# Queries and keys of a forgetting attention as pairs of float16, scaled by powers of two, on one core

## The chip, the core and the metric

The kernel runs on one core of one Trainium2 chip. The metric is the device time of one execution in microseconds (us). A core has five engines with a queue of instructions each: TensorE (PE, matmuls into PSUM), VectorE (DVE), ScalarE (ACT), GpSimd (POOL) and SyncE (SP, which issues DMAs here). An engine takes its instructions in order and waits on semaphores for the others.

## The reference

One layer for 2048 tokens of width 1024. A projection of the modulated RMSNorm gives queries, keys and values of 8 heads of 64 columns, a forget logit for each head, and the inputs of a gated short convolution. The change touches the attention alone:

```python
    q = rmsnorm(q.reshape(b, s, ATTN_HEADS, HEAD_DIM), q_norm_g)
    k = rmsnorm(k.reshape(b, s, ATTN_HEADS, HEAD_DIM), k_norm_g)
    logf = jax.nn.log_sigmoid((fg + b_forget).astype(jnp.float32))
    ...
    fcum = jnp.cumsum(logf, axis=1)            # per head
    for i in range(s // BLOCK_Q):              # 16 blocks of 128 queries
        logits = jnp.einsum('bqhd,bkhd->bhqk', qb, kb).astype(jnp.float32) * scale
        logits = logits + fcum[:, :, q0:q1, None] - fcum[:, :, None, :q1]
        logits = jnp.where(causal[None, None], logits, -jnp.inf)
        p = jax.nn.softmax(logits, axis=-1).astype(v.dtype)
        outs.append(jnp.einsum('bhqk,bkhd->bqhd', p, vb))
```

After it come the output projection, a second norm, and a feed-forward layer with a convolution (`w_up` to 5632 columns, `w_down` back).

## The kernel before

Everything is held to float32 accuracy by pairs: a number is split into a high part and the rest, both in a 4-byte matmul type (float32r), and a product is made of three matmuls, high by high, high by rest, rest by high (`mm3`, L139).

**Projections** (about 40 to 620 us of the span). The values come first. Then `project` runs twice, for the keys and for the queries. It goes over 16 tiles of 128 tokens: 24 matmuls (8 slices of the width, three each), then a norm for each head on ACT and DVE. `finish` of a tile comes two tiles later: PE transposes the tile (L462), ACT multiplies with the gain `gq` into `tf` (L468), POOL copies it to the high part `th`, DVE subtracts to get the rest `tl`, and SP stores both in DRAM (`k_hi`, `k_lo`, `q_hi`, `q_lo`). Small steps hang on the tiles as `hooks`: `running_sum` and `running_offset` for the cumulated forget gates (`cum`, stored as `nf_sc`), `largest_value` and `value_scale` for the scale of the values. After the queries come the convolution's projections (`pr`).

**Attention** (626 to about 970 us). `load_head` fetches a head: the keys' high part (`kh`) and rest (`kl`), 64 partitions each, which POOL copies to the other 64 partitions, and the queries' two parts, one above the other in `qs`; so one matmul with `qs` as the loaded weights gives high and rest of the queries at once. The work goes by units: one head and two query blocks, number 15 - u and u, for u from 0 to 7, which have 17 key blocks of 128 together. There are 64 units. For a unit

- `product` makes the scores on PE in chunks of up to 512 columns, five for a unit: one matmul with `kh` (L658), one with `kl` (L659), and for the last chunk of a block the causal mask (L661). It always issues two chunks at a time (GROUP), across the units;
- `scores` adds the forget term `nf` on DVE and finds the running maximum (L682, the output is `s_t`, 17 blocks wide);
- `weights` makes the bias `nb` from the maximum (L696) and takes the exponential of the two blocks on ACT, with their sums (L699);
- `turn` splits the result in two f16 parts and transposes it: seven key blocks by POOL (`wide`) and a transposing DMA (`far`), ten by PE (L719, into two PSUM buffers `pt`), ACT (`near`, L721) and DVE (`near`, L726);
- `values` multiplies with the values in f16 (L751 to L753), 64 columns a matmul, and ACT scales the result (`at`, L757).

The loop at the end of the part advances four units by one step each in turn: `turn` of the unit two before, `scores` of this one, `weights` of the one before, `values` of the one four before. PE, ACT and DVE are pinned to the order that is written so (`K`); SP's queue is placed by the framework.

Of the kernel before, what the change touches and what calls it, by code (L numbers as in the profile page):

```python
# [19 lines left out]
P = 128  # L20
S = 2048
D = 1024
H = 8
DH = 64
AW = 512
# [7 lines left out]
LN_PS = 9.704060527839234  # L33
# [11 lines left out]
def kernel(  # L45
# [19 lines left out]
    nc = tc.nc  # L65
    V, A, G, T = nc.vector, nc.scalar, nc.gpsimd, nc.tensor
# [4 lines left out]
    const = ctx.enter_context(tc.tile_pool(name="const", bufs=1))  # L71
# [5 lines left out]
    q_lo = dram.tile([P, 4, S], F32, name="q_lo")  # L77
    k_hi = dram.tile([P, 4, S], F32, name="k_hi")
    k_lo = dram.tile([P, 4, S], F32, name="k_lo")
# [66 lines left out]
    with ExitStack() as ph:  # L146
# [256 lines left out]
        def running_offset():  # L403
            po = ps_t.tile([P, 512], F32, tag="tr", name="po")
            K(T.matmul(po[:, 0:1], lhsT=blk.rearrange("p h t -> p (h t)"), rhs=cum[:, P - 1 : P], start=True, stop=True))
            off = bp.tile([P, 1], F32, name="off", bufs=1)
            V.tensor_copy(off, po[:, 0:1])
            V.tensor_scalar(cum, cum, off, -1.0, op0=ALU.add, op1=ALU.mult)
            nc.scalar.dma_start(nf_sc.rearrange("h (t k) -> (h t) k", k=P), cum)

        vr = bp.tile([1, 1], F32, name="vr", bufs=1)

# [43 lines left out]
        def project(col, gain, dst_hi, dst_lo, hooks):  # L456
            w = [w_slice(w_in[k * P : (k + 1) * P, col : col + AW], [P, AW]) for k in range(KD)]

            def finish(i, qn):
                pt = ps_t.tile([P, 512], F32, tag="tr", name="pt")  # L460
                for j in range(4):
                    K(T.transpose(  # L462
                        pt[:, j * P : (j + 1) * P], qn[:, 2 * j : 2 * j + 2, :].rearrange("p h d -> p (h d)"), ident
                    ))
# [3 lines left out]
                A.activation(tf, pt, AF.Copy, scale=gain)  # L468
                pool_copy(th, tf)
                V.tensor_tensor(tl, tf, th.bitcast(F32), op=ALU.subtract)  # L470
                for dst, src in ((dst_hi, th), (dst_lo, tl)):
                    nc.sync.dma_start(
                        dst[:, :, i * P : (i + 1) * P], src.bitcast(F32).rearrange("p (j n) -> p j n", j=4)
                    )

            normed = []
            for i in range(NT):
                ch, t = divmod(i, 4)
                acc = ps_m.tile([P, 512], F32, tag="mm", name="acc")
                for k in range(KD):  # L480
                    ah, al = h_hi[k][ch][:, t * P : (t + 1) * P], h_lo[k][ch][:, t * P : (t + 1) * P]
                    mm3(acc, ah, al, w[k][0], w[k][1], k == 0, k == KD - 1)
                    if k == MID and len(normed) == 2:
                        finish(*normed.pop(0))
                a3 = acc.rearrange("p (h d) -> p h d", d=DH)
                sq = bp.tile([P, 512], F32, tag="z", name="sq")
                A.activation(sq, acc, AF.Square)
# [12 lines left out]
            def finish_last():  # L500
                finish(*normed.pop(0))
                if col == 0 and not normed:
                    value_tiles(NT)

            return finish_last
# [44 lines left out]
                taken[1] += 1  # L550

        taken = [0, 0]
        last_k = project(AW, gq[:, 1:2], k_hi, k_lo, {3: running_sum, 5: running_offset, 7: largest_value, 9: value_scale})
        last_q = project(0, gq[:, 0:1], q_hi, q_lo, {0: last_k, 1: last_k, 3: piece, 6: piece, 9: piece, 12: piece, 15: piece})

        def load_head(h):

            pr, r0 = h // 2, (h % 2) * DH
            r1 = r0 + DH
            tiles, steps = [], []  # L560
            load = lambda *a: steps.append(lambda: nc.sync.dma_start(*a))
            for tag, srcs in (("kh", (k_hi,)), ("qs", (q_hi, q_lo)), ("kl", (k_lo,))):
                t = sp.tile([P, S], F32R, tag=tag, name=tag)
                for n, src in enumerate(srcs):
                    load(t.bitcast(F32)[n * DH : (n + 1) * DH, :], src[r0:r1, pr, :])
                tiles.append(t)
            t = sp.tile([P, S], F32, tag="nf", name="nf")
            load(t, nf_sc[h].partition_broadcast(P))
            for k in (tiles[0], tiles[2]):
                steps.append(lambda k=k: K(G.tensor_scalar(k[DH:P, :], k.bitcast(F32)[0:DH, :], 1.0, 0.0, op0=ALU.mult, op1=ALU.add)))  # L570
            return (*tiles, t), steps


# [47 lines left out]
    with ExitStack() as ph:  # L621
# [70 lines left out]
        def weights(un):  # L692

            s_t = un["s"]
            nb = cs.tile([P, 2], F32, tag="nb", name="nb")
            K(A.activation(nb, un["mx"], AF.Copy, scale=-1.0, bias=LN_PS))  # L696
            for p, (_, n, b0) in enumerate(un["parts"]):
                cols = s_t[:, b0 * P : (b0 + n) * P]
                K(A.activation(cols, cols, AF.Exp, bias=nb[:, p : p + 1], accum_out=un["l"][:, p : p + 1]))  # L699
# [492 lines left out]
```

## Time and profile before

| | |
|---|---|
| median of 3 runs | 2540.8 us (2540.46 to 2541.75) |
| the profiled execution | 2540.43 us, its span from first to last instruction 2538.7 us |
| PE, DVE, ACT, POOL busy | 2454.4, 1823.9, 1169.9, 359.4 us |
| granted clock of TensorE, mean | 0.993 |
| attention, 620 to 970 us of the span | PE 341.3, DVE 297.1, ACT 293.9, POOL 210.0 us busy |

An engine is busy while one of its instructions runs. Matmuls are pipelined: a row gives the time from a matmul's start to its modelled end, and the next one starts before that, so the rate is read from the starts. `<-` behind an idle time names what ended it.

### The profile page before, as it was taken

What the parts mean: (1) busy time and instruction counts of PE and PEld (TensorE: products, weight loads), DVE (VectorE), ACT (ScalarE), POOL (GpSimd) and SP (SyncE); (2) the same over time, 40 slices, a digit from 0 to 9 for tenths busy, and PEclk for the clock granted to TensorE, in tenths of its full rate; (3) what the DMA queues carried; (4) which work ended last, traced back from release to release, by engine and by line L of the source; (5) the groups of instructions that cost most, each with busy time, mean ns of one, the idle gap of its engine ahead of it and who ended that gap; (6) DMA issues with size and microseconds to landing.
All of it is one profiled execution on the core that took longest, in us unless ns stands there. A gap on an engine that the chain in (4) does not pass through costs nothing.

```text
span 2538.7 us, 38468 instructions
## 1 busy us (share of the span) xinstructions
PE 2454.4 (97%) x14490; PEld 2027.5 (80%) x14490; DVE 1823.9 (72%) x3282; ACT 1169.9 (46%) x1932; POOL 359.4 (14%) x314
## 2 busy tenths in 40 slices
PE   4999999999999997998999999999999999999999
PEld 4988788887788886876888888877778888888887
DVE  7567874433888886676888888667768888885554
ACT  3532331111888885654444444455534444444333
POOL 4210111101666655110000000000000000000000
PEclk9999999999999999999999999999999999999999
DMA  7433673325799867143222222676642222226775
GB/s 233 147 107 102 195 224 98 98 63 148 140 198 193 165 130 245 63 150 103 75 84 83 83 83 83 209 229 213 223 136 78 83 84 83 83 85 198 228 234 184
DMA packets 400290, 358.21 MB, mean 141 GB/s; under 512 B 133776, under 2 KB 310248, under 8 KB 397032
## 3 DMA queue, kind: packets, MB, share of 16 engines
q1 hardware_dynamic: 392920, 338.91, 46.6%
q10 hardware_dynamic: 4752, 8.46, 0.9%
q0 software_dynamic: 2432, 8.39, 0.9%
q8 instruction: 113, 1.85, 0.3%
q14 instruction: 73, 0.60, 0.1%
HBM read 252.86 MB, written 73.47 MB: 129 GB/s over the span
## 4 chain that ended last, share of the span: by engine, by line
PE 49%; DVE 2%; DMA 1%; ACT 1%; issue 0%; SPq 0%; ACTq 0%; DVEq 0%
PE acc L1044 33%; PE acc L139 16%; DMA t<-x_sc 1%; DVE lo L843 1%; PE pt L932 0%; DVE t L852 0%; DVE t L925 0%; DVE t L851 0%; ACT junk L955 0%; ACT hi L842 0%; DMA raw<-y_sc 0%; DVE b22l L843 0%; DVE lo L999 0%; DVE t L942 0%; ACT t L934 0%
## 5 line engine op out<-in xcount | busy, mean ns | idle before, releaser
L139 PE MATMUL acc<-hi 128*128 128x512 f32 x960 | 378.0, 394 | 15.9 <-ACT hi L842 12.3
L139 PE MATMUL acc<-hi,lo 128*128 128x512 f32 x960 | 375.7, 391 | 0.2 <-DVE lo L843 0.2
L139 PE MATMUL acc<-lo,hi 128*128 128x512 f32 x960 | 374.9, 391 | 0.0
L843 DVE TENSOR_TENSOR lo<-raw,hi 128x1024 fp32r<-128x1024 f32 (+1 forms) x208 | 236.0, 1141 | 182.5 <-ACT hi L842 182.2
L842 ACT ACTIVATE hi<-raw 128x1024 fp32r<-128x1024 f32 (+1 forms) x208 | 205.0, 991 | 247.7 <-PE acc L139 203.0
L1057 DVE SCALAR_TENSOR_TENSOR w<-w,fcw,w 128x1024 f32<-128x1024 f32 x176 | 225.9, 1283 | 35.5 <-ACT w L1052 32.2
L996 ACT ACTIVATE hi<-raw 128x1024 fp32r<-128x1024 f32 x132 | 139.7, 1060 | 213.4 <-PE acc L1044 204.7
L139 PEld LDWEIGHTS acc<-hi 128*128 128x128 f32 x960 | 180.9, 188 | 56.5 <-ACT hi L842 13.2
L139 PEld LDWEIGHTS acc<-hi,lo 128*128 128x128 f32 x960 | 180.6, 188 | 39.9 <-DVE lo L843 2.0
L139 PEld LDWEIGHTS acc<-lo,hi 128*128 128x128 f32 x960 | 180.9, 188 | 36.7 <-DVE lo L843 0.4
L999 DVE TENSOR_TENSOR lo<-raw,hi 128x1024 fp32r<-128x1024 f32 x132 | 160.9, 1220 | 11.0 <-ACT hi L996 10.9
L699 ACT ACTIVATE s_t<-s_t,nb 128x2048 f32<-128x2048 f32 (+15 forms) x128 | 152.9, 1196 | 5.7
L139 PE MATMUL pr<-hh,wh 128*128 128x512 f32 x384 | 153.3, 399 | 0.0
L139 PE MATMUL pr<-hl,wh 128*128 128x512 f32 x384 | 151.1, 393 | 0.0
L139 PE MATMUL pr<-hh,wl 128*128 128x512 f32 x384 | 150.8, 393 | 0.0
L726 DVE TENSOR_TENSOR near<-pt,near 128x512 f16<-128x512 f32 (+1 forms) x192 | 114.8, 599 | 44.7 <-ACT near L721 43.8
L658 PE MATMUL ps<-kh,qs 128*128 128x512 f32 (+1 forms) x320 | 133.6, 418 | 1.0 <-issue 0.8
L682 DVE CUSTOM_DVE_ANT_0 s_t<-ps,nf,mx 128x512 f32<-128x512 f32 (+1 forms) x192 | 123.2, 641 | 3.0 <-PE pt L719 0.4
L711 POOL TENSOR_TENSOR wide<-s_t,wide 128x896 f16<-128x896 f32 x64 | 121.7, 1901 | 5.3
L659 PE MATMUL ps<-kl,qs 128*128 128x512 f32 (+1 forms) x320 | 115.5, 365 | 0.0
L719 PE MATMUL pt<-ident,s_t 128*128 128x128 f32 x640 | 101.0, 283 | 7.6 <-DVE near L726 5.3
L139 PE MATMUL acc<-wh,hh 128*128 128x512 f32 x256 | 103.4, 404 | 0.0
(287 smaller groups left out, 6263.8 us busy)
## 6 DMA issues: line engine op xcount, KB each, us to landing
raw<-in_w_up_dram SPq DMA_DIRECT2D x88, 512.0 KB, 3.6
raw<-y_sc SPq DMA_DIRECT2D x176, 256.0 KB, 3.9
raw<-in_w_down_dram SPq DMA_DIRECT2D x176, 256.0 KB, 4.2
y_sc<-w SPq DMA_DIRECT2D x44, 512.0 KB, 2.6
wm<-in_w_ada_dram SPq DMA_DIRECT2D x128, 128.0 KB, 2.3
wr<-in_w_in_dram SPq DMA_DIRECT2D x40, 256.0 KB, 4.0
x_t<-in_x_dram SPq DMA_DIRECT2D x16, 512.0 KB, 5.4
wa<-in_w_ada_dram SPq DMA_DIRECT2D x16, 512.0 KB, 6.4
```

The source lines that it names most:

```text
L139: ins = T.matmul(acc, lhsT=a, rhs=b, start=st, stop=sp)
L658: K(T.matmul(ps[:, 0:cw], lhsT=qt, rhs=kh[:, c0 : c0 + cw], start=True, stop=False))
L659: K(T.matmul(ps[:, 0:cw], lhsT=qt, rhs=kl[:, c0 : c0 + cw], start=False, stop=not last))
L682: K(V.tensor_tensor_reduce(out=s_t[:, o0 + c0 : o0 + c0 + cw], in0=ps[:, 0:cw], in1=nf[:, c0 : c0 + cw], scale=1.0, scalar=-3.0e38 if g == ...
L699: K(A.activation(cols, cols, AF.Exp, bias=nb[:, p : p + 1], accum_out=un["l"][:, p : p + 1]))
L711: K(G.tensor_tensor(wide[:, 1, :], s_t[:, WB * P : WU], wide[:, 0, :], op=ALU.subtract))
L842: A.activation(hi, raw, AF.Copy, scale=HS)
L843: V.tensor_tensor(lo, raw, hi.bitcast(F32), op=ALU.subtract)
L996: K(A.activation(hi, raw, AF.Copy, scale=HS))
L999: K(V.tensor_tensor(lo, raw, hi.bitcast(F32), op=ALU.subtract))
L1044: K(T.matmul(acc, lhsT=a, rhs=b, start=st, stop=sp, skip_group_check=True))
L1057: K(V.scalar_tensor_tensor(y, u[:, m : m + 1024], fcw[:, m * 44 + ct : m * 44 + ct + 1], y, op0=ALU.mult, op1=ALU.add))
```

## The change

Queries and keys are kept as pairs of float16. Each gain is multiplied by a power of two that is found from the largest gain, and the product of the two scales is multiplied into the forget term. The logits stay scaled, and the exponential divides by the product of the scales, held in `qk`: column 4 is its reciprocal, column 5 the negative of that, column 3 the product.

```diff
-    q_hi = dram.tile([P, 4, S], F32, name="q_hi")
+    q_hi = dram.tile([P, 4, S], F16, name="q_hi")
...
+    qk = const.tile([P, 6], F32, name="qk")
...
             V.tensor_scalar(cum, cum, off, -1.0, op0=ALU.add, op1=ALU.mult)
+            V.tensor_scalar(cum, cum, qk[:, 3:4], None, op0=ALU.mult)
...
+        def largest_gains():
+            pt = ps_t.tile([P, 512], F32, tag="tr", name="pt")
+            K(T.transpose(pt[0:2, 0:P], gq, ident))
+            V.tensor_reduce(gm[:, 0:1], pt[0:2, 0:P], axis=AX.X, op=ALU.max, apply_absolute_value=True)
+            V.tensor_scalar(gm, ident[0:2, 0:2], gm[:, 0:1], 8.0, op0=ALU.mult, op1=ALU.mult)
+
+        def gain_scales():
+            pt = ps_t.tile([P, 512], F32, tag="tr", name="pt")
+            K(T.matmul(pt[:, 0:2], lhsT=ones[0:2, :], rhs=gm, start=True, stop=True))
+            s = qk[:, 0:2]
+            V.tensor_scalar(s, pt[:, 0:2], 2.0**-10, 2.0**60, op0=ALU.max, op1=ALU.min)
+            V.tensor_scalar(s.bitcast(I32), s.bitcast(I32), 0x7F800000, None, op0=ALU.bitwise_and)
+            V.reciprocal(s, s)
+            V.tensor_scalar(s.bitcast(I32), s.bitcast(I32), 0x7F800000, None, op0=ALU.bitwise_and)
+            V.tensor_scalar(s, s, 16384.0, None, op0=ALU.mult)
+            V.tensor_tensor(gq, gq, s, op=ALU.mult)
+            V.tensor_tensor(qk[:, 3:4], s[:, 0:1], s[:, 1:2], op=ALU.mult)
+            V.reciprocal(qk[:, 4:5], qk[:, 3:4])
+            V.tensor_scalar(qk[:, 5:6], qk[:, 4:5], -1.0, None, op0=ALU.mult)
...
-                th = bp.tile([P, 512], F32R, tag="th", name="th")
-                tl = bp.tile([P, 512], F32R, tag="tl", name="tl")
+                th = bp.tile([P, 512], F16, tag="th", name="th")
+                tl = bp.tile([P, 512], F16, tag="tl", name="tl")
...
-        last_k = project(AW, gq[:, 1:2], k_hi, k_lo, {3: running_sum, 5: running_offset, 7: largest_value, 9: value_scale})
+        last_k = project(AW, gq[:, 1:2], k_hi, k_lo, {0: largest_gains, 1: gain_scales, 3: running_sum, 5: running_offset, 7: largest_value, 9: value_scale})
...
-                t = sp.tile([P, S], F32R, tag=tag, name=tag)
+                t = sp.tile([P, S], F16, tag=tag, name=tag)
...
-            K(A.activation(nb, un["mx"], AF.Copy, scale=-1.0, bias=LN_PS))
+            K(A.activation(nb, un["mx"], AF.Copy, scale=qk[:, 5:6], bias=LN_PS))
...
-                K(A.activation(cols, cols, AF.Exp, bias=nb[:, p : p + 1], accum_out=un["l"][:, p : p + 1]))
+                K(A.activation(cols, cols, AF.Exp, bias=nb[:, p : p + 1], scale=qk[:, 4:5], accum_out=un["l"][:, p : p + 1]))
```

`q_lo`, `k_hi` and `k_lo` become float16 as `q_hi` does, and the stores and loads follow. The program's instructions stand as follows. First PE at the start of the attention, before and now:

```order
L658 MATMUL ps<-kh,qs 128x512
L659 MATMUL ps<-kl,qs 128x512
L658 MATMUL ps<-kh,qs 128x128
L659 MATMUL ps<-kl,qs 128x128
L661 LDWEIGHTS ident_b
L661 MATMUL ps<-maskb,ident_b 128x128
```

```order
L682 LDWEIGHTS qs
L682 MATMUL ps<-kh,qs 128x512
L683 LDWEIGHTS qs
L683 MATMUL ps<-kl,qs 128x512
L682 LDWEIGHTS qs
L682 MATMUL ps<-kh,qs 128x128
L683 LDWEIGHTS qs
L683 MATMUL ps<-kl,qs 128x128
L685 LDWEIGHTS ident_b
L685 MATMUL ps<-maskb,ident_b 128x128
```

No matmul moved; the load of the weights stands as an instruction of its own, 640 of them in all. Next ACT in the first unit of the attention, before and now:

```order
L696 ACTIVATE nb<-mx 128x2
L699 ACTIVATE s_t,l<-s_t,nb 128x2048
L699 ACTIVATE s_t,l<-s_t,nb 128x128
L721 ACTIVATE near<-pt 128x512 x2
L696 ACTIVATE nb<-mx 128x2
```

```order
L720 ACTIVATE nb<-mx,qk 128x2
L723 ACTIVATE s_t,l<-s_t,nb,qk 128x2048
L723 ACTIVATE s_t,l<-s_t,nb,qk 128x128
L745 ACTIVATE near<-pt 128x512 x2
L720 ACTIVATE nb<-mx,qk 128x2
```

The order is the same, and each of the three reads `qk` besides. Last SP, where the second next head is fetched between the transposing DMAs, before and now:

```order
L712 DMA_TRANSPOSE far<-wide 128x14x128 x6
L561 DMA kh<-k_hi 64x2048
L712 DMA_TRANSPOSE far<-wide 128x14x128
L561 DMA qs<-q_hi 64x2048
L712 DMA_TRANSPOSE far<-wide 128x14x128
L561 DMA qs<-q_lo 64x2048
L561 DMA kl<-k_lo 64x2048
```

```order
L736 DMA_TRANSPOSE far<-wide 128x14x128 x6
L585 DMA kh<-k_hi 64x2048
L585 DMA qs<-q_hi 64x2048
L736 DMA_TRANSPOSE far<-wide 128x14x128
L585 DMA qs<-q_lo 64x2048
L585 DMA kl<-k_lo 64x2048
```

The load of `q_hi` and what follows it stand one transpose earlier; later the stores of the attention's output stand one place later in turn. On POOL the copy of the first head's `kl` stands one instruction (`y`, L614) earlier. DVE has twelve instructions more, those of the diff, in the key projection.

More of the change, by code (lines that the diff above doesn't have):

```diff
@@ L74 @@
     dram = ctx.enter_context(tc.tile_pool(name="dram", bufs=1, space=DRAM))
-    q_hi = dram.tile([P, 4, S], F32, name="q_hi")
-    q_lo = dram.tile([P, 4, S], F32, name="q_lo")
-    k_hi = dram.tile([P, 4, S], F32, name="k_hi")
-    k_lo = dram.tile([P, 4, S], F32, name="k_lo")
+    q_hi = dram.tile([P, 4, S], F16, name="q_hi")
+    q_lo = dram.tile([P, 4, S], F16, name="q_lo")
+    k_hi = dram.tile([P, 4, S], F16, name="k_hi")
+    k_lo = dram.tile([P, 4, S], F16, name="k_lo")
     v_sc = dram.tile([S, AW], F32, name="v_sc")
@@ L408, in running_offset @@
             V.tensor_scalar(cum, cum, off, -1.0, op0=ALU.add, op1=ALU.mult)
+            V.tensor_scalar(cum, cum, qk[:, 3:4], None, op0=ALU.mult)
             nc.scalar.dma_start(nf_sc.rearrange("h (t k) -> (h t) k", k=P), cum)
+        gm = bp.tile([2, 2], F32, name="gm", bufs=1)
+        def largest_gains():
[16 more added lines that the diff above has]
+            V.tensor_scalar(qk[:, 5:6], qk[:, 4:5], -1.0, None, op0=ALU.mult)
         vr = bp.tile([1, 1], F32, name="vr", bufs=1)
@@ L562, in load_head @@
             for tag, srcs in (("kh", (k_hi,)), ("qs", (q_hi, q_lo)), ("kl", (k_lo,))):
-                t = sp.tile([P, S], F32R, tag=tag, name=tag)
+                t = sp.tile([P, S], F16, tag=tag, name=tag)
                 for n, src in enumerate(srcs):
-                    load(t.bitcast(F32)[n * DH : (n + 1) * DH, :], src[r0:r1, pr, :])
+                    load(t[n * DH : (n + 1) * DH, :], src[r0:r1, pr, :])
                 tiles.append(t)
@@ L569, in load_head @@
             for k in (tiles[0], tiles[2]):
-                steps.append(lambda k=k: K(G.tensor_scalar(k[DH:P, :], k.bitcast(F32)[0:DH, :], 1.0, 0.0, op0=ALU.mult, op1=ALU.add)))
+                steps.append(lambda k=k: K(G.tensor_scalar(k[DH:P, :], k[0:DH, :], 1.0, 0.0, op0=ALU.mult, op1=ALU.add)))
             return (*tiles, t), steps
```

6 lines of the change are left out of this document (2 added, 4 removed).

## The prediction

> **What bounds the kernel now.** I read the page first: the share of each engine, then the costliest groups, to find what the changed lines carry.
>
> ```profile
> span 2538.7 us, 38468 instructions
> PE 2454.4 (97%) x14490; PEld 2027.5 (80%) x14490; DVE 1823.9 (72%) x3282; ACT 1169.9 (46%) x1932; POOL 359.4 (14%) x314
> ```
>
> TensorE (PE) is busy for 97% of the span, ScalarE (ACT) for 46%. That is an average. The products of queries and keys stand in the attention alone, so the second view is the table by stretches there. I took 48 of its 64 units (a unit is one pair of query blocks of one head), from one `nb` instruction to the same one six heads later, and the waits in the same stretch.
>
> ```profile
> 670.20 0.21 ACT L696 ACTIVATE nb<-mx 128x2 f32<-128x2 f32 x1
> 925.74 0.21 ACT L696 ACTIVATE nb<-mx 128x2 f32<-128x2 f32 x1
> ...
> 670.20:925.74 255.54, 252.54 (x3554) 208.43 (x3553) 220.51 (x673) 221.40 (x494) 159.24 (x109) 1.00 0.91 180
> ...
> POOL wide L710 <- ACT s_t L699: 91.0, 45, 3.1
> DVE near L726 <- ACT near L721: 32.3, 48, 1.1
> ACT at L757 <- PE po L753: 19.2, 27, 1.1
> PEld pt L719 <- DVE near L726: 8.3, 31, 0.5
> ACT near L721 <- PE pt L719: 6.4, 39, 0.2
> ACT tm L767 <- PE pt L765: 1.7, 6, 0.3
> PE pt L719 <- DVE near L726: 1.6, 5, 0.4
> ```
>
> The columns of the stretch are PE, weight loads, DVE, ACT and POOL in us, then clock, DMA share and rate. A unit takes 255.54/48 = 5.32 us. PE is busy for 252.5 of 255.5 us at a granted clock of 1.00, so PE sets the time. But ACT is close behind: 221.4 us busy, and of its 34.1 idle us it waits for PE during 19.2 + 6.4 + 1.7 = 27.3. The other 6.8 are its own small gaps. Without waits for PE a unit would cost ACT (221.4 + 6.8)/48 = 4.75 us. The third view, ACT in order of time, shows that this happens:
>
> ```profile
> 760.13 0.20 ACT L696 ACTIVATE nb<-mx 128x2 f32<-128x2 f32 x1
> 764.48 0.32 ACT L757 ACTIVATE at<-po,l 128x64 f32<-128x64 f32 x1 [1.10 <-PE po L753]
> 765.92 0.21 ACT L696 ACTIVATE nb<-mx 128x2 f32<-128x2 f32 x1
> 770.76 0.20 ACT L696 ACTIVATE nb<-mx 128x2 f32<-128x2 f32 x1
> ```
>
> One unit takes 5.79 us with 1.1 us of waiting for PE, the next 4.84 us without such a wait. The two kinds alternate, because `product` issues score chunks two at a time and a unit has five: PE gets six chunks in one unit and four in the next. So the long units are PE's and the short ones are already ACT's. With an average of 5.32, short ones near 4.80 and long ones near 5.8 are the picture to change.
>
> **The change, part by part.**
>
> *Score products, PE.* 320 matmuls on L658 and 320 on L659 keep their columns; both operands go from 4-byte to 2-byte types.
>
> ```profile
> L658 PE MATMUL ps<-kh,qs 128*128 128x512 f32 x224 | 101.0, 451 | 1.0 <-issue 0.8 <-DVE mx L682 0.2
> L659 PE MATMUL ps<-kl,qs 128*128 128x512 f32 x224 | 88.3, 394 | 0.0
> L658 PE MATMUL ps<-kh,qs 128*128 128x384 f32 x32 | 13.5, 422 | 0.0
> L659 PE MATMUL ps<-kl,qs 128*128 128x384 f32 x32 | 10.7, 334 | 0.0
> ...
> L658 PEld LDWEIGHTS ps<-kh,qs x320: 186/190/204, 626.1 to 958.9; 128*128 128x128 f32 x160
> L751 PEld LDWEIGHTS <-near x640: 95/98/101, 644.1 to 971.5; 128*128 128x128 f16 x160
> ...
> 763.26 0.40 PE L659 MATMUL ps<-kl,qs 128*128 128x512 f32 x1
> 763.49 0.39 PE L658 MATMUL ps<-kh,qs 128*128 128x512 f32 x1
> 763.72 0.39 PE L659 MATMUL ps<-kl,qs 128*128 128x512 f32 x1
> ...
> 764.04 0.19 PE L752 MATMUL po<-v,far 128*128 128x64 f16 x1
> 764.07 0.19 PE L753 MATMUL po<-v,far 128*128 128x64 f16 x1
> ```
>
> Two savings are seen here. First, the 512-column kh matmul shows 451 ns against 394 for kl: 57 ns x 224 = 12.8 us, a weight load (190 ns) that isn't hidden when it follows the short value matmuls. The same difference on the 96 narrower chunks, 422 against 334 ns where it is largest, adds some 4 us: 17 us in all. The f16 weight load of the value products takes 98 ns, and these start 30 ns apart at 64 columns, so f16 loads hide even there. Second, steady f32 matmuls start 230 ns apart at 512 columns, which is 0.45 ns a column. An f16 row of 64 columns takes 30 ns; how much of this is fixed the trace doesn't say. At worst (nothing fixed) 512 columns take 235 ns and the second saving is nil. At best, an estimate, PE takes 0.42 ns a column and 3 ns fixed, which gives the 30: then the 278,528 columns of all 640 (17,408 for a head and matmul, from the causal lengths) take 117 + 2 = 119 us, while in the order of time the steps from the 640 starts (the first at 626.1, as in the L658 row) to PE's next start add up to 150. The ends are 17 and 31 us; I take 28, since the f16 rows show no cost of loads. That is 0.44 us a unit, 0.53 in a unit with six chunks. The 640 separate LDWEIGHTS that the order now shows are not new work: the profile of before has a load for each of them too.
>
> The Trainium skill speaks against part of this: its page "TensorE: Matmul & The Clock Gate", section "Back-to-back issue gap", gives about 81 ns for a load and matmul of 128 columns in a stream, against 56 for a matmul alone, so a load would keep costing some 25 ns. By that, 640 x 25 = 16 us of the saving would be gone and the sum would be rival C below; the 30 ns of the f16 pairs in this trace speak against it.
>
> *The exponential, ACT.* The scale of the 128 `Exp` (L699) becomes a column of `qk`, beside the column of the bias; the 64 `nb` (L696) get a column in place of a constant. Rows with none, one and two such columns:
>
> ```profile
> L487 ACT ACTIVATE sq<-acc 128x512 f32<-128x512 f32 x32 | 19.1, 597 | 114.4 <-PE acc L139 114.4
> L468 ACT ACTIVATE tf<-pt,gq 128x512 f32<-128x512 f32 x32 | 21.8, 682 | 0.0
> L272 ACT ACTIVATE hf<-pt,sh,a 128x512 f32<-128x512 f32 x32 | 24.6, 778 | 17.9 <-PE pt L270 11.2 <-DVE hl L274 4.3 <-ACT vt L347 1.4
> L244 ACT ACTIVATE sh<-pmod,cst 128x1 f32<-128x1 f32 x8 | 2.1, 262 | 29.2 <-PE pmod L241 29.2
> L245 ACT ACTIVATE a<-pmod,bg,cst 128x1 f32<-128x1 f32 x8 | 2.8, 344 | 0.0
> L699 ACT ACTIVATE s_t<-s_t,nb 128x2048 f32<-128x2048 f32 x8 | 16.0, 2006 | 0.7
> ```
>
> The first column costs 85 ns, the second 82 to 96. So 128 x 0.09 + 64 x 0.085 = 17.0 us more on ACT, 0.27 us a unit (ends: 0, if an Exp with sums takes it for nothing, and 18.4). By the Trainium skill, "ScalarE: Activation LUTs", section "What ACT_TABLE_LOAD costs", each such operand adds about 93 ns; by that alone it would be 17.9 us. No row here has an `Exp` with both.
>
> *What the stage comes to.* ACT's floor rises from 4.75 to 5.02 us a unit. PE's long units fall from 5.8 to 5.27; some of their excess can be taken back in the short ones, where PE, at four chunks, now ends well before ACT. With all of it taken back every unit costs 5.02; with none, (5.02 + 5.27)/2 = 5.15. I take 5.08: 64 x (5.32 - 5.08) = 15.4 us less. DVE needs 220.5/48 = 4.59 us a unit and POOL 3.32, so they stay under it; DVE's wait for ACT's `near` grows, and costs nothing while ACT is the bound. Once PE no longer sets the pace, ACT is late next.
>
> *Projections.* `th` and `tl` in f16: the same instructions, the DMAs at half the bytes (k_hi and the like, in pieces of 256 bytes). PE covers them: it is busy for all but 1 us of 120 there. Two small PE instructions come in, after tiles 0 and 1 of the keys; a like pair stands at 216.94:
>
> ```profile
> 180.00:300.00 120.00, 118.95 (x562) 96.91 (x561) 94.70 (x345) 32.32 (x54) 12.46 (x20) 1.00 0.46 137
> ...
> 216.41 0.60 PE L462 MATMUL pt<-ident,qn 128*128 128x128 f32 x4
> 216.94 0.38 PE L422 MATMUL pt<-vr,ones 1*128 1x1 f32 x2
> 217.24 0.50 PE L139 MATMUL acc<-wh,hh 128*128 128x512 f32 x1
> ...
> 193.26 0.15 DVE L407 COPY off<-po 128x1 f32<-128x1 f32 x1
> 193.92 0.35 DVE L408 TENSOR_SCALAR cum<-cum,off 128x128 f32<-128x128 f32 x1
> ...
> L570 POOL TENSOR_SCALAR kl<-kl 64x2048 fp32r<-64x2048 f32 x8 | 15.6, 1951 | 0.7
> ```
>
> 0.3 to 0.4 us each, on PE's path: +0.7. Their eleven DVE instructions (0.15 to 0.2 us each like L407, 2 us in all) run while PE does the 24 matmuls of the next tile, 24 x 0.23 = 5.5 us; `finish` of tile 0 needs the gains only a tile later. If that cover failed, the first `tf` would be 1 to 2 us late and PE still has two tiles in hand. The extra `cum` on DVE (0.35 us, as L408's) is hidden too.
>
> *Loads.* Heads are fetched in half the bytes, the two POOL copies a head stay (1.95 us each on L570, half as much at best, on an engine that is busy for 159 of 255 us), and on SyncE's queue the loads stand one transpose earlier than before. The DMA share of 0.91 falls. A transpose that is pushed back by one issue is needed two units later, some 10 us: nothing. POOL takes the first head's kl copy ahead of one `y` (L614) of the last convolution; PE doesn't read that `y`.
>
> Sum against the profiled execution, 2540.4 us: - 15.4 + 0.7 = 2525.7. The median of the runs lies 0.4 us above it: **2526 us**.
>
> **Rivals.**
>
> A, the forecast: ACT becomes the bound at 5.02 to 5.15 a unit, 2522 to 2531. Chance 0.54.
>
> B, the pointer column on `Exp` costs little or nothing. ACT stays at 4.75 to 4.85, PE's long units at 5.2: a unit takes about 4.95, 64 x 0.37 = 24 us less, 2517; with PE at its best end 2510. Against it: every pair of rows above shows the cost. Chance 0.16.
>
> C, f16 matmuls take off only the exposed loads, 17 us or less: a long unit loses 0.32 and stays PE's at 5.48, a short one is 5.02; 5.25 on average, 4.5 us less, 2536 with the added work; with part of the rest 2532. Chance 0.14.
>
> D, slower. Long units are not set by PE's work but by a ring: ACT's `near` releases DVE's `near` (L726), which frees the PSUM buffer that PE's transposes (L719) wait for, which ACT's next `near` waits for. Exps that are longer by 0.27 us push this ring round in every unit. For it: the 32.3 us in which DVE waits for `near`. Against: PE waits for L726 during 8.3 + 1.6 us of 255 only. Short units lose 0.27 in any case, so the kernel is slower as soon as long ones gain less than 0.27 of their 0.53. If they gain nothing of it, up to 64 x 0.27 = 17 us; half of that gives 2549. Chance 0.07.
>
> E, the two effects meet: within 0.2% (5 us), about what measurements of this kernel can tell from no change. Chance 0.09.
>
> **How the numbers follow.** A, B and nearly all of C (0.12) lie more than 5 us below 2540.8: 0.82 faster; the same 0.11 with C's rest; slower 0.07. The range takes in A, most of B and of C: 2513 to 2538. The likeliest case by itself reaches from 2522 to 2531.
>
> **What the new profile would show.** The kh and kl rows both under 390 ns with no gap between them, and starts at most 220 ns apart at 512 columns: else the PE term is wrong. `Exp` of 2048 columns at 2.10 us instead of 2.01, and `nb` at 0.29 instead of 0.20: else the ACT term is. ACT's wait on `po` near zero, ACT busy for over 95% of the stretch, and PE with idle time before its transposes: else the change of bound is. `nb` to `nb` near 5.05 in long and short units alike; if long ones stay above 5.4, C or D holds. I would be most wrong if DVE, at 4.59 a unit, can't hide its own waits on ACT: then units end nearer to 5.3.

## The result and the profile after

The change makes the kernel slower: 2562.1 us (2560.33 to 2565.62, 4 runs) against 2541.2 for the kernel before on the same chip, a ratio of 1.0084 (95% interval 1.0067 to 1.0102). The forecast was 2526. Both terms of the forecast for the attention, PE's saving and ACT's cost, were measured at nearly their forecast size. But in the time of the attention they cancelled, and a third effect, of which the prediction has no word, cost the 21 us elsewhere.

**Where the 21 us are.** First the head of the page after. TensorE, granted clock 0.992, is as busy as before in share, and longer in us, although the new score matmuls are shorter.

```profile
span 2560.5 us, 38478 instructions
PE 2458.1 (96%) x14493; PEld 1995.7 (78%) x14493; DVE 1820.9 (71%) x3294; ACT 1183.2 (46%) x1932; POOL 357.8 (14%) x314
```

The table by stretches, cut down to the matmuls of the feed-forward layer's first product (L1044 before, L1068 after; the line is the same code), shows where. Columns: stretch, length, PE busy (count), weight loads, clock, DMA share, rate. Before:

```profile
1100.00:2400.00 1300.00, 850.21 (x3696) 697.61 (x3696) 0.99 0.39 126
1400.00:1550.00 150.00, 150.00 (x660) 123.59 (x659) 1.00 0.26 83
```

After:

```profile
1100.00:2400.00 1300.00, 871.22 (x3696) 697.74 (x3696) 0.99 0.39 123
1400.00:1550.00 150.00, 150.00 (x645) 120.60 (x644) 1.00 0.25 81
```

The same 3696 matmuls take 21.0 us more. In 150 us without a gap, at a clock of 1.00 both times, PE runs 660 of them before and 645 after: 227.3 and 232.6 ns each. In order of time, eight steps from one of these matmuls to a later one, before and after:

```profile
1500.01 0.39 PE L1044 MATMUL acc<-b11h,hi 128*128 128x512 f32 x1
...
1501.82 0.39 PE L1044 MATMUL acc<-b11h,lo 128*128 128x512 f32 x1
```

```profile
1499.98 0.40 PE L1068 MATMUL acc<-t3l,hi 128*128 128x512 f32 x1
...
1501.85 0.40 PE L1068 MATMUL acc<-b22h,hi 128*128 128x512 f32 x1
```

That is 1.81/8 = 226 ns against 1.87/8 = 234. No line of the diff touches this layer. What did change is where its tiles lie: `qk` is a new tile of 24 bytes a partition in the pool `const`, its place is rounded up to 32, and everything that is laid out behind it moves up by 32 bytes, `b11h` for one from address 89088 to 89120 in each partition. The experiments below test this.

**The attention** is as long as before: from one `nb` to the same one six heads later, 255.40 us against 255.54. But what fills it is different. The row of that stretch (PE, weight loads, DVE, ACT, POOL) and its waits, after:

```profile
671.19:926.59 255.40, 238.47 (x3553) 184.45 (x3552) 219.63 (x673) 231.48 (x493) 158.68 (x109) 1.00 0.78 155
...
DVE near L750 <- ACT near L745: 33.9, 50, 1.1
PEld pt L743 <- DVE near L750: 23.6, 48, 0.9
PE pt L743 <- DVE near L750: 14.9, 36, 0.7
ACT near L745 <- PE pt L743: 9.8, 45, 0.3
ACT at L781 <- PE po L777: 8.3, 21, 0.6
```

PE has 14 us less to do and gives them back in waits: its transposes (L743) now wait 14.9 us for DVE's `near`, where it was 1.6, and their weight loads 23.6 instead of 8.3. ACT has 10 us more to do and waits less for PE. The groups of the changed instructions:

```profile
L682 PE MATMUL ps<-kh,qs 128*128 128x512 f16 x224 | 84.9, 379 | 2.0 <-ACT bt L635 1.1 <-DVE mx L706 0.9
L683 PE MATMUL ps<-kl,qs 128*128 128x512 f16 x224 | 84.9, 379 | 0.0
...
L723 ACT ACTIVATE s_t<-s_t,nb,qk x128: 477/1288/2097, 631.2 to 964.9; 128x2048 f32<-128x2048 f32 x8, 128x128 f32<-128x128 f32 x8, 128x1920 f32<-128x1920 f32 x8, 128x256 f32<-128x256 f32 x8
L720 ACT ACTIVATE nb<-mx,qk x64: 287/297/298, 630.8 to 963.1; 128x2 f32<-128x2 f32 x64
```

The kh and kl matmuls are alike now at 379 ns, so no weight load shows any more; the longest `Exp` takes 2097 ns, `nb` 297. The alternation is still there; ACT in order of time, and a wait of PE that falls between the last two rows:

```profile
761.75 0.30 ACT L720 ACTIVATE nb<-mx,qk 128x2 f32<-128x2 f32 x1
765.88 0.31 ACT L781 ACTIVATE at<-po,l 128x64 f32<-128x64 f32 x1 [0.60 <-PE po L777]
767.32 0.30 ACT L720 ACTIVATE nb<-mx,qk 128x2 f32<-128x2 f32 x1
772.34 0.29 ACT L720 ACTIVATE nb<-mx,qk 128x2 f32<-128x2 f32 x1
...
771.15 0.66 PE L743 MATMUL pt<-ident,s_t 128*128 128x128 f32 x4 [0.68 <-DVE near L750]
```

One unit takes 5.57 us, the next 5.02. The long one still has a wait for PE in it; the short one is longer than it was. PE stands before its transposes near the end of the short unit, and in its order the score matmuls that follow wait behind them. Of the 14.9 us of this wait, 10.6 fall into the short units, between the `nb` of an even-numbered unit and the next `nb`, and 4.3 into the long ones.

### The profile page after: what moved, and what is told of

The parts are those of the page before. It is cut to its first block, busy times and chain, and to the rows that moved or that the text cites. A ratio compares the mean times of both kernels' runs of the same rounds, so it can differ in the third digit from the quotient of the medians.

```text
span 2560.5 us, 38478 instructions
## 1 busy us (share of the span) xinstructions
PE 2458.1 (96%) x14493; PEld 1995.7 (78%) x14493; DVE 1820.9 (71%) x3294; ACT 1183.2 (46%) x1932; POOL 357.8 (14%) x314
## 4 chain that ended last, share of the span: by engine, by line
PE 50%; DVE 2%; DMA 1%; ACT 1%; issue 0%; SPq 0%; DVEq 0%; ACTq 0%
PE acc L1068 34%; PE acc L140 16%; DMA t<-x_sc 1%; DVE lo L867 1%; PE pt L956 0%; DVE t L949 0%; DVE t L876 0%; DVE t L875 0%; ACT junk L979 0%; ACT hi L866 0%; DVE b22l L867 0%; DVE lo L1023 0%; DVE t L966 0%; ACT t L958 0%; DVE w L986 0%
## 5 line engine op out<-in xcount | busy, mean ns | idle before, releaser
L1023 DVE TENSOR_TENSOR lo<-raw,hi 128x1024 fp32r<-128x1024 f32 x132 | 161.0, 1221 | 10.7 <-ACT hi L1020 10.6
L723 ACT ACTIVATE s_t<-s_t,nb,qk 128x2048 f32<-128x2048 f32 (+15 forms) x128 | 164.7, 1288 | 5.8
L743 PE MATMUL pt<-ident,s_t 128*128 128x128 f32 x640 | 102.1, 284 | 26.2 <-DVE near L750 24.2
L682 PE MATMUL ps<-kh,qs 128*128 128x512 f16 (+1 forms) x320 | 109.9, 347 | 2.0 <-ACT bt L635 1.1
L683 PE MATMUL ps<-kl,qs 128*128 128x512 f16 (+1 forms) x320 | 109.6, 347 | 0.0
```

Source lines behind the costliest of these rows:

```text
L682: K(T.matmul(ps[:, 0:cw], lhsT=qt, rhs=kh[:, c0 : c0 + cw], start=True, stop=False))
L723: K(A.activation(cols, cols, AF.Exp, bias=nb[:, p : p + 1], scale=qk[:, 4:5], accum_out=un["l"][:, p : p + 1]))
L1023: K(V.tensor_tensor(lo, raw, hi.bitcast(F32), op=ALU.subtract))
```

## The experiments

Two questions were put: does the place of the tiles make the 21 us, and why is the attention not shorter? "Unscaled" kernels keep the float16 pairs and leave out the scaling by powers of two. The kernel before, run along with each, took between 2539.9 and 2541.5 us.

### Is it the 32 bytes?

Once with the change and no move (`qk` in six unused columns of the constants `cst`), once with the move and no change:

```diff
-    qk = const.tile([P, 6], F32, name="qk")
+    qk = cst[:, 96:102]
```

> The changed kernel, but qk lies in unused columns of the tile cst, so that no SBUF tile moves. In the changed kernel qk took 32 bytes a partition and every tile after it in the left stack lies 32 bytes further; the operands of the feed-forward matmuls (b11h, t1h and so on) then start 32 bytes past a multiple of 64. Address theory: the feed-forward steps go back from 234 to 227 ns and the 20 us come back; the attention stays where it is, so 2541 (2537 to 2545). Rival, the float16 tensors in DRAM (other sizes, other places) or the later start of the feed-forward part slow it: stays at 2562. Rival, the attention itself was slowed by the 32 bytes too: under 2535.

```diff
+    pad = const.tile([P, 6], F32, name="pad")
+    V.memset(pad, 0.0)
```

> The kernel before with one unused tile of 6 columns where the change put qk (written once, never read), so all left tiles lie 32 bytes further; nothing else. Address theory: 2562 (2558 to 2566), with the feed-forward matmuls at 234 ns from start to start and the attention at 5.32 us a unit. Rival, DRAM places or float16: 2541.

Measured: 2538.2 us for the first, ratio to before 0.9999 (0.9990 to 1.0009), and 2561.4 for the second, 1.0087 (1.0072 to 1.0102). The unused tile alone makes the kernel before as slow as the changed one, and without the move of the tiles the change costs nothing. In the 150 us from 1400 us on there are 660 and 645 of the matmuls. The attention takes 5.321 us a unit in the first, as after, and 5.320 in the second: the place of tiles does nothing there.

### Which addresses are good ones?

A pad of 64 bytes in the kernel before, then `qk` as a tile of 128, 256 and 512 bytes:

```diff
+    pad = const.tile([P, 16], F32, name="pad")
```

> The kernel before with an unused tile of 64 bytes a partition where the change put qk, so all left tiles lie 64 bytes further. If the feed-forward matmuls need operands at multiples of 64: 2541 (2538 to 2544), 227 ns from start to start. If at multiples of 128, or if the mere place matters: 2555 to 2562.

```diff
-    qk = const.tile([P, 6], F32, name="qk")
+    qk = const.tile([P, 32], F32, name="qk")
```

> The changed kernel with qk as a tile of its own of 128 bytes a partition in place of 24, so that every tile behind it moves by 128 bytes and not by 32. Theory: what costs is the operands' address modulo 128 bytes. Then the feed-forward matmuls are back at 227 ns and the time is that of qk in columns of cst, 2538 us (2535 to 2543). Rival: it is the move itself or the tile's presence (other tiles, other neighbours), 2557 to 2566.

(and 64 or 128 in place of 32)

> The changed kernel with qk as a tile of 256 bytes a partition, so that every tile behind it moves by 256 bytes. Moves by 32, 64 and 128 bytes slowed the feed-forward matmuls to 233, 231 and 232 ns a step. If it is the moving operand's address modulo 512 bytes that counts, 256 is still wrong: 2546 to 2560 us. If modulo 256, they are back at 227 ns: 2538 us (2535 to 2543). If any move from the old addresses costs, 2550 to 2566.

> The changed kernel with qk as a tile of 512 bytes a partition: every tile behind it moves by 512 bytes, and the operands of the feed-forward keep their place modulo 512. Theory: 227 ns a step again and 2538 us (2535 to 2543). Rival: any move from the old addresses costs (a larger modulus, other neighbours), 2550 to 2566.

The sum in the table is over 3690 steps, from the start of one of these matmuls to that of the next where nothing else of PE's stands between.

| moved by, bytes | kernel | sum of the steps, us | in 1400 to 1550 us | median, us | ratio (95%) |
|---|---|---|---|---|---|
| 0 | before | 856.7 | 660 | 2541.2 | |
| 32 | after | 877.6 | 645 | 2562.1 | 1.0084 (1.0067 to 1.0102) |
| 64 | before, pad | 869.3 | 645 | 2545.2 | 1.0019 (1.0004 to 1.0033) |
| 128 | `qk` of 128 bytes | 872.7 | 648 | 2554.4 | 1.0058 (1.0043 to 1.0073) |
| 256 | `qk` of 256 bytes | 857.1 | 660 | 2540.9 | 1.0002 (0.9992 to 1.0011) |
| 512 | `qk` of 512 bytes | 857.2 | 661 | 2540.8 | 1.0003 (0.9993 to 1.0012) |

The rows of the 128 and the 256 bytes:

```profile
1400.00:1550.00 150.00, 150.00 (x648) 121.66 (x647) 1.00 0.26 81
```

```profile
1400.00:1550.00 150.00, 150.00 (x660) 123.62 (x659) 1.00 0.26 85
```

My first theory, 64 bytes, fell with the first of these runs, and the second, 128 bytes, with the next; both times lay between the two that had been expected. Of the moves tried, those that are multiples of 256 bytes are free and the others are not. With 64 bytes the time rose by less than the steps, and the runs lie far apart (2539.65 to 2554.84); the rest of that is not explained.

### Whose addresses are they?

The pool of the feed-forward has two fillers already, `rim` of 128 bytes at its start and `rim2` of 384 further on. In the changed kernel, once the first and once the second is made 32 bytes shorter:

```diff
-        fp.tile([P, 32], F32, name="rim")
+        fp.tile([P, 24], F32, name="rim")
```

> The changed kernel with qk as a tile of its own, and the filler rim at the start of the pool fp cut from 128 to 96 bytes a partition: all tiles of the feed-forward stand where they stood before, those of the projections and of the attention stay moved by 32 bytes. If only the feed-forward's addresses count: 227 ns a step and 2538 us (2535 to 2543), as with qk in columns of cst. If the move of the earlier parts costs too: 2545 to 2562.

```diff
-                fp.tile([P, 96], F32, name="rim2")
+                fp.tile([P, 88], F32, name="rim2")
```

> The changed kernel with the second filler, rim2, cut from 384 to 352 bytes in place of the first: of the moving operands of the feed-forward all stand where they stood before except t1h, t1l and t2h, which stay moved by 32 bytes, as the sources src and the wide temporaries w4 do. If the matmul's own operand counts, steps with b11, b21, b22, t3, t4 and t2l are back at 227 ns and those with t2h stay at 233: 2541 us (2537 to 2546). If the tiles that DVE and ACT use (src, w4) cause it by what they take from PE, all operands stay at 233: 2558 to 2566.

Measured 2542.2 us, 1.0008 (0.9998 to 1.0018), and 2544.4, 1.0016 (1.0007 to 1.0026). So the move of the projections' and the attention's tiles costs little, 2 us by the medians, which the interval doesn't separate from nothing, and the feed-forward's own tiles are what counts. The second kernel shows it matmul by matmul (count, then min/median/max in ns, first and last start; the first name behind the arrow is the moving operand of 512 columns, the second the loaded weights, which never moved and in this layer all start at multiples of 256 bytes):

```profile
L1068 PE MATMUL acc<-b11h,hi x176: 389/389/628, 1177.4 to 2277.6; 128*128 128x512 f32 x176
...
L1068 PE MATMUL acc<-t2h,hi x176: 389/398/504, 1185.1 to 2280.4; 128*128 128x512 f32 x176
L1068 PE MATMUL acc<-t2l,hi x176: 389/393/393, 1185.5 to 2280.6; 128*128 128x512 f32 x176
L1068 PE MATMUL acc<-t2h,lo x176: 392/394/502, 1185.7 to 2280.9; 128*128 128x512 f32 x176
L1068 PE MATMUL acc<-b21h,hi x176: 388/389/703, 1190.8 to 2283.1; 128*128 128x512 f32 x176
```

`t2h` is still moved by 32 bytes there, and the product with it is slow, `t2l` included, which stands between two of its matmuls and is itself at a multiple of 256. All others but `t1`, which is moved too, are back at 389. The rival, that tiles of DVE and ACT take something from PE, would have slowed all.

### Does the rule predict forward?

One moving operand, `t1l`, stood at 64 modulo 256 in the kernel before already, and the product with `t3`, which follows and is itself at multiples of 256, was slow with it. 192 bytes of filler move ahead of it, in two kernels that are described further down:

```diff
+            if Q == 1:
+                fp.tile([P, 48], F32, name="rim1")
...
-                fp.tile([P, 96], F32, name="rim2")
+                fp.tile([P, 48], F32, name="rim2")
```

> The whole change with qk in columns of cst and score chunks one at a time (2534.0 us), and 192 bytes of filler moved from rim2 to a place ahead of t1l: the one moving operand of the feed-forward that stood at 64 modulo 256 bytes before (t1l) now stands at 0. If the address modulo 256 counts, the steps with t1h, t1l and t3 (229.9, 232.5, 231.5, 230.8 and 232.2 ns in the kernel before) go to 226.7: (3.2 + 5.8 + 4.8 + 4.1 + 5.5) x 176 = 4.1 us less, 2530 us (2527 to 2533). Rival: those steps have another cause (they stand where PE's output changes buffers), no change, 2532 to 2536.

> Unscaled pairs with score chunks one at a time (2518.8 us; the scaling by powers of two is left out) with the same 192 bytes of filler ahead of t1l. By the address modulo 256: 2514.7 us (2512 to 2517). Rival: no change, 2517 to 2521.

The same matmuls without and with the filler, in the first of the two. `t3` has not moved:

```profile
L1068 PE MATMUL acc<-t1h,hi x176: 387/394/478, 1187.6 to 2278.1; 128*128 128x512 f32 x176
L1068 PE MATMUL acc<-t1l,hi x176: 388/394/398, 1187.9 to 2278.3; 128*128 128x512 f32 x176
...
L1068 PE MATMUL acc<-t3h,hi x176: 388/394/479, 1190.8 to 2280.8; 128*128 128x512 f32 x176
```

```profile
L1070 PE MATMUL acc<-t1h,hi x176: 389/389/478, 1190.9 to 2276.8; 128*128 128x512 f32 x176
L1070 PE MATMUL acc<-t1l,hi x176: 389/389/393, 1191.2 to 2277.0; 128*128 128x512 f32 x176
...
L1070 PE MATMUL acc<-t3h,hi x176: 389/389/478, 1194.1 to 2279.5; 128*128 128x512 f32 x176
```

The median step is 227 ns for every product of the layer now, and the sum of the steps falls from 857.8 to 852.8 us (856.9 to 854.1 in the second). The kernels take 2531.9 us, 0.9961 (0.9949 to 0.9974), and 2515.6, 0.9900 (0.9885 to 0.9915). Against the same kernels without the filler that is 2 and 3 us less, which the intervals don't separate; the steps do. In the kernel before, the first eight of the twelve steps with `t3` are the slow ones, 224 to 236 ns, and the last four are at 227. So a misplaced operand acts on matmuls some way behind it. Why `t3` is at 227 in the kernel with the shorter `rim2`, where `t1` is slow too, is open.

### Why the attention gains nothing

One half of the change at a time: float16 without the scaling, and the scale columns alone in the kernel before. The first kernel has no `qk` and none of the steps that fill it; the diff against the changed kernel shows only the two lines on ACT.

```diff
-            K(A.activation(nb, un["mx"], AF.Copy, scale=qk[:, 5:6], bias=LN_PS))
+            K(A.activation(nb, un["mx"], AF.Copy, scale=-1.0, bias=LN_PS))
...
-                K(A.activation(cols, cols, AF.Exp, bias=nb[:, p : p + 1], scale=qk[:, 4:5], accum_out=un["l"][:, p : p + 1]))
+                K(A.activation(cols, cols, AF.Exp, bias=nb[:, p : p + 1], accum_out=un["l"][:, p : p + 1]))
```

> Float16 pairs without any scale: no qk, gains as before, exponential and nb with constants as before, and no tile moved. It leaves out the scaling by powers of two. Theory, the attention stood still because ACT's longer instructions took what PE saved: with ACT's rows as before a unit falls to 4.95 to 5.05 us, 64 x 0.3 = 18 us less than before: 2521 (2516 to 2527). Rival, a ring of ACT, DVE and PE holds the unit at 5.3 whatever PE or ACT cost: 2540.

In the second kernel the two lines stand the other way round, with 1.0 and -1.0 in two columns of `cst`:

> The kernel before (float32r pairs) with only the two scale columns: the exponential takes a column of ones and nb a column of -1, both in unused columns of cst, no tile moved. Theory, ACT bounds the short units and PE the long ones: short units 4.75 to 5.02, long ones nearly unchanged, 64 x 0.14 = 9 us more: 2550 (2547 to 2554). Rival, the ring: every unit pays 0.27, 17 us more: 2558. Rival, ACT has slack: 2541.

Measured 2531.8 us, 0.9966 (0.9956 to 0.9976), and 2547.6, 1.0030 (1.0017 to 1.0042). The distance from the `nb` of unit u to the next, mean over the six heads of the stretch above, in us:

| | mean | u = 0 | 1 | 2 | 3 | 4 | 5 | 6 | 7 |
|---|---|---|---|---|---|---|---|---|---|
| before | 5.324 | 5.12 | 5.71 | 4.76 | 6.02 | 4.99 | 5.47 | 4.75 | 5.77 |
| float16 alone | 5.189 | 5.12 | 5.48 | 4.76 | 5.69 | 4.98 | 5.14 | 4.75 | 5.59 |
| columns alone | 5.448 | 5.37 | 5.66 | 5.02 | 6.00 | 5.26 | 5.47 | 5.03 | 5.77 |
| both (`qk` in `cst`) | 5.321 | 5.37 | 5.44 | 5.02 | 5.71 | 5.26 | 5.14 | 5.02 | 5.60 |

This is the account. Each half acts on its own kind of unit and leaves the other: float16 takes 0.27 us off the long ones (u odd), the columns add 0.27 to the short ones (u even). By the means, -0.135 and +0.124 a unit, and together -0.003. I had expected 2521 us from float16 alone, with all units near 5; that part of my theory fell. What holds the long units at 5.5 then? The waits of the float16 kernel:

```profile
PEld pt L718 <- DVE near L725: 18.9, 42, 0.7
ACT at L756 <- PE po L752: 13.5, 25, 0.9
PE pt L718 <- DVE near L725: 11.0, 31, 0.5
```

PE stands before its transposes until DVE has emptied their buffer, again more in the short units (6.3 us) than in the long ones (4.7). Two ways to act on that: issue score chunks one at a time (GROUP = 1 in place of 2), so that PE's work is spread evenly, or put the last two blocks' transposes one round later in `turn`.

```diff
-GROUP = 2
+GROUP = 1
```

> Unscaled float16 pairs with GROUP = 1: product issues one chunk of scores at a time, so PE has five chunks in every unit in place of six and four in turn. It leaves out the scaling by powers of two. Theory, the long units are set by PE's part of a path over two units, of which the sixth chunk is 0.43 us: units even out and come to 4.95, 64 x 0.24 = 15 us under the kernel with GROUP = 2 (2532): 2517 (2512 to 2524). Rival, DVE's part of the path sets the long units, and PE's chunks do not matter: 2530 to 2533.

> The changed kernel with qk in cst and GROUP = 1. Same theory, with the scale columns on ACT: its floor of 5.02 us a unit holds, units at 5.1, so 64 x 0.22 = 14 us under 2540: 2526 (2521 to 2532). Rival as before: 2537 to 2541.

> The kernel before with GROUP = 1 alone. With float32r every single chunk follows short value matmuls, so its kh load is exposed for each of 320 chunks in place of about 200: some 120 x 0.085 = 10 us more on PE, which is the bound, against the evening of the units. Theory: 2540 to 2550, no gain without float16. Rival, the gain of GROUP = 1 has nothing to do with float16: under 2532.

| GROUP = 1 in | us a unit, with 2 | with 1 | median, us | ratio (95%) |
|---|---|---|---|---|
| before | 5.324 | 5.233 | 2532.4 | 0.9961 (0.9946 to 0.9976) |
| the change, `qk` in `cst` | 5.321 | 5.221 | 2534.0 | 0.9974 (0.9964 to 0.9985) |
| float16, unscaled | 5.189 | 5.024 | 2518.8 | 0.9912 (0.9898 to 0.9927) |

All three gain. The second ends at 2534.0 us, 2 us outside the range that I gave. The kernel before gains too, which I had not expected, though there every kh matmul now follows short value matmuls and its load is exposed nearly each time (315 ns from kh to kl, the median at 512 columns). The waits in the unscaled kernel:

```profile
ACT at L756 <- PE po L752: 6.6, 24, 0.5
PE pt L718 <- DVE near L725: 4.2, 15, 0.5
```

PE's wait falls from 11.0 to 4.2 us, and ACT's for `po` by half. The two kinds of unit come together: the even ones take 4.99 us and the odd ones 5.06, where GROUP = 2 had 4.90 and 5.48. Then the later transposes:

```diff
             blocks(0)
             blocks(4)
             yield
             rest()
             yield
-            blocks(8)
             rest()
             yield
+            blocks(8)
             rest()
```

> It leaves out the scaling by powers of two (as the unscaled pairs before it, 2531.8 us, 5.19 us a unit), and in turn PE's transposes of the last two blocks stand one round later, behind the second rest(). My theory: a long unit ends late because PE, which takes its instructions in order, stands at these transposes until DVE's rest() has freed the PSUM buffer, with the next unit's score matmuls queued behind them. With the transposes later the buffer is free when PE comes to them: the long units fall from 5.44 to about 5.0, 32 x 0.4 = 13 us less: 2519 us (2514 to 2524), and PE's wait for near L725 in the stretch falls from 11 us to under 3. Rival 1: the long units are set by PE's own work or by ACT's wait for po; nothing changes, 2530 to 2534. Rival 2: near, and with it the values and the release of buffers, comes a round later and the units grow: over 2536.

> Unscaled pairs with the score chunks issued one at a time (2518.8 us, 5.02 us a unit), and besides the transposes of the last two blocks one round later. If the wait for DVE's rest() is what is left above ACT's floor of 4.75 and PE's work of some 4.93 a unit, units go to about 4.93: 64 x 0.09 = 6 us less, 2513 us (2509 to 2517). If PE's work alone sets them, no change: 2517 to 2521. If near comes too late for ACT and the values: over 2523.

> The whole change with qk in columns of cst, score chunks one at a time (2534.0 us, 5.22 us a unit), and the transposes of the last two blocks one round later. ACT's floor is 5.02 with the two pointer columns. If the wait for DVE's rest() is the rest, units go to about 5.04: 64 x 0.18 = 11 us less, 2523 us (2519 to 2528). If the units above the floor (numbers 1, 3 and 7 of each head) have another cause, 2531 to 2537.

Measured 2530.1 us, 0.9964 (0.9952 to 0.9977), for the first (2531.8 without); 2524.4, 0.9940 (0.9926 to 0.9955), for the second (2518.8); 2540.2, 1.0002 (0.9993 to 1.0011), for the third (2534.0). The first kernel's waits:

```profile
ACT at L756 <- PE po L752: 11.6, 24, 0.7
...
PE pt L718 <- DVE near L725: 9.5, 24, 0.6
...
PE ps L657 <- DVE mx L681: 1.9, 6, 0.3
```

So my theory, that the place of these transposes in PE's order makes the wait, fell. In the first kernel PE's wait fell to 9.5 us and not to under 3; the long units lost 0.14 us and the short ones gained as much, 5.190 us a unit against 5.189. With GROUP = 1 the kernels lose 6 us. Issuing the chunks two at a time is shown to make the long and short units and to cost 0.09 to 0.17 us a unit; since GROUP = 1 also issues each chunk later, how much of that is the unevenness alone is not shown. Which single wait holds the rest of the long units is left open; moving one step only moved the wait.

## Why the prediction was wrong, by its own steps

- **Score products, 28 us.** Right. The steps from the 640 starts add up to 121.4 us after, 150.0 before: 28.6 less, waits included. 512 columns take 216 ns in float16, and kh and kl have the same row, so no load is exposed. Rival C, 17 us or less, falls. (The worst end of the working is slightly off: 30 ns for 64 columns would be 240 ns for 512, not 235. Nothing hangs on it.) The Trainium skill, "TensorE: Matmul & The Clock Gate", section "Back-to-back issue gap", gives about 81 ns for a load and matmul of 128 columns in a stream, from which the prediction worked out 25 ns a load; in this trace such pairs start 56 ns apart, so it is not borne out here.
- **ACT's columns, 17.0 us.** Right: the 128 `Exp` take 164.7 us instead of 152.9, the 64 `nb` 0.09 us more each, 17.6 in all. Rival B falls. The Trainium skill, "ScalarE: Activation LUTs", section "What ACT_TABLE_LOAD costs", gives about 93 ns for such an operand; the trace agrees, (164.7 - 152.9)/128 = 92 ns.
- **Projections, +0.7 us.** Right: the first kh matmul is at 626.8 us in the trace after, at 626.1 before. No wait for the heads' loads stands among the waits of the attention, as said.
- **What the stage comes to, -15.4 us.** Wrong; it came to -0.2. The step that failed is "PE's long units fall from 5.8 to 5.27; some of their excess can be taken back in the short ones": the long ones fell by 0.27 (5.74 to 5.47, the rows "before" and "both" of the table), not by the 0.53 that the step gives them even with nothing taken back. The short units rose by 0.27, as forecast, and the four long and four short units of a head cancel. The step took a unit as the longer of PE's work and ACT's work, and PE as free to work ahead in the short units. But PE waited 14.9 us for DVE's `near`, 1.6 before, and 10.6 of them in the short units, where it should have worked ahead. That this wait alone accounts for the missing 0.26 is argued, not shown; see the later transposes. The last sentence of the prediction names DVE's waits on ACT as what would make it most wrong ("then units end nearer to 5.3"), and rival D names the ring through `near`; neither was given weight enough, since PE's wait was small in the trace before. Rival D's time, half of 17 us, didn't come; its condition ("as soon as long ones gain less than 0.27") is the balance at which the attention landed. That it landed so near to zero is chance: two effects of 0.27 us, each on its own kind of unit.
- **What was missing, +21 us.** The change was costed where it acts. A new tile in a pool that is laid out ahead of all the others was not counted as a part of the change at all, and no rival has it. In the kernel before, the unused tile alone makes 20.8 us (2540.6 to 2561.4), and the change without the move takes 2538.2. Two signs were there: the fillers `rim` and `rim2` in the pool of the feed-forward, tiles that nothing reads, and the product with `t1l`, at 64 modulo 256, whose steps in the trace before were 230 to 233 ns where the aligned ones of this layer had 227.
- **What the profile would show.** Rows under 390 ns, 216 ns steps, 2.10 us and 0.29 us: seen. ACT busy over 95% and no wait for `po`: not seen (90.6%; 8.3 us). Long units above 5.4: seen, and the reading given for it, "C or D holds", was right in D's part.

The float16 pairs with GROUP = 1 and `t1l` moved, at 2515.6 us, are the fastest version run, but they leave out the scaling. The whole change in that form takes 2531.9; both beat the kernel before.

## What to carry to other kernels

A new tile, however small, is a change to every tile behind it: compare the addresses of the matmul operands, moving and loaded, before and after, put small additions into spare columns of a tile that is there, and take a filler tile in a tuned kernel as a warning. Where two engines take turns at being late, a saving on one acts in its own units only, and is not taken against the other's floor; look which buffer the freed engine will wait for. An A/B of a small change says little about the change until a kernel with the unused allocation alone has been run.

## What the runs showed of the hardware

In the feed-forward's first product, whose loaded weights all start at multiples of 256 bytes in the partition, a float32r matmul of 128 x 512 takes 226.7 ns a step if its moving operand starts at such a multiple too. These are means of the product with `t4`, some 176 steps for each of its three pairs of operands. The same three take 233.4 ns at 32 bytes past a multiple, 229.6 to 232.5 at 64 and 230.6 to 233.9 at 128, up to 3% more. A neighbour in the stream at a bad address slows it as well (`t2l` above, 232.5 ns).

The moving operand's address is not the whole rule. The convolution's projections (`pr`) are float32r matmuls of 128 x 512 as well, and in their first two token chunks the moving operand starts at a multiple of 256 in every kernel and never moves. Their mean step is 231.3 ns in the kernel before all the same, 233.3 to 233.4 in the three kernels whose loaded weights there stand 32 bytes further (the changed one, the unused tile, the shorter `rim`), and 231.1 in those whose weights stand 64, 128 or 256 bytes further. With the weights at 0, 64, 128 and 192 modulo 256 the median steps are 228, 233, 232 and 229 ns in the kernel before; in the other two chunks, with the moving operand at 128, they are 232, 229, 227 and 233. So the place of the loaded operand counts too, and here the pairs with the same remainder are the fastest. Even that is no general rule: in the key and query projections such pairs take 233 ns, and in the attention before, where `kh`, `kl` and `qs` all start at multiples of 256, the steps within a run of score products at 512 columns are at 231 to 232 (medians). None of the runs tried to place the operands of the projections better, so what that would gain is open.

No effect of the place was seen in the attention, whose units kept their time to 0.004 us when the tiles moved; `kh`, `kl` and `qs` are not among those that did. The Trainium skill, "SBUF — State Buffer", section "Operand start alignment", asks for a multiple of the element's size and says that it is about legality, not speed; the runs show the speed. Why 256 bytes, the runs don't tell. And float16 matmuls with a weight load each start 216 ns apart at 512 columns, 163 at 384, 109 at 256, 56 at 128 and 29 at 64.
